# Differential attention: the output norm on other engines, its transposes later, the last head's products last

## The chip, the core and the metric

One kernel, one launch, on one core of a Trainium2 chip. TensorE (PE) multiplies and transposes into PSUM, which has eight banks of 128x512 float32 here; VectorE (DVE) and ScalarE (ACT) read PSUM and SBUF, GpSimd (POOL) only SBUF; SyncE (SP) issues every DMA of this kernel, in one queue. Each engine runs its instructions in the order in which they stand in the program. The metric is the device time of one execution in microseconds, the median of some runs.

## What is computed

One decoder layer: a normalised input is projected once, three branches (a convolution module, differential attention, cross-attention into memory tokens) are each gated and projected to the model width, summed under sigmoid gates, and projected once more. The change touches the differential attention and what follows it:

```python
def one_block(args):                       # 128 query rows, all 8 heads, two maps m of width 64
    ...
    p = jax.nn.softmax(s, axis=-1)
    a = (p[:, :, 0] - lam * p[:, :, 1]).astype(vt.dtype)
    return jnp.einsum("bhqk,bhkd->bhqd", a, vt)
...
o = rms_norm(o, subln_g) * (1.0 - lambda_init)       # per head, 128 wide
o = o.reshape(B, S, DIFF_WIDTH) * jax.nn.silu(gate)
return o @ w_proj
...
y = g[:, :, 0] * y_conv + g[:, :, 1] * y_diff + g[:, :, 2] * y_mem
x = x + y @ w_out[l]
```

SEQ and D_MODEL are 1024, there are 8 heads. All is float32; each large product is made of three passes on float32r halves (high x high, low x high, high x low), the helper `mm3` on lines 78 to 80.

## The kernel before

The instructions of PE stand in the order in which the Python code writes them; those of the other engines and of SP are ordered by a scheduler, by priority and by its own estimate of times. A tile pool with `bufs=n` gives n buffers to a name in turn, and an instruction that takes a buffer again waits for the last reader.

**Attention** (lines 974 to 1369). The work is cut into 32 groups: 8 heads, and in each head four blocks `g` of 256 query rows in the order 2, 3, 0, 1. A group has these steps on PE, each with its helpers on other engines:

- scores (L1045, L1047) into two `sc` banks; DVE adds the distance and takes the maximum (L1051), DVE and ACT do the softmax (L1062 to L1069). `rc` is one over the sum of each map, and POOL copies its first column to `r` (the tile `r0`, L1071);
- transposes of the weights (L1089) into one of three `tp` banks, copied out by ACT (L1091);
- products with the values (L1097) into the one `av` bank, copied to the tile `o` by ACT (L1102);
- the output norm (L1106 to L1116): ACT sums squares (L1111), then the helper `rstd_of` makes one over the root: POOL L173, ACT L174 and L175, POOL L176 to L179, then POOL L1114 multiplies by `r`, and DVE scales `o` (L1116);
- the turn (L1118 to L1135): PE transposes `o` into a `tp` bank (L1123), ACT copies it out with a scale (L1126), POOL multiplies it by the gate `gd` (L1127), which a DMA fetched. For heads 0 to 3 the result is split into a high and a low half for the products below, for heads 4 to 7 it goes to memory (L1129).

At the start of each head POOL also makes the low halves of keys and queries (L1012) for the next one, and it makes low halves of weights (L113).

A planner walks a model of the engines' times and writes PE's steps in that order; `CHAIN` is the time that it allows between the squares of the norm and the scaled `o`, in its own units. Where no step is ready it inserts fill: six matmuls at a time of independent projections into two `mm` banks, evicted by DVE (L1162, L1191). So the fill's amount is fixed, and only its place moves.

**The end** (lines 1371 to 1418). The rest of the fill comes first, while the outputs of heads 4 to 7 are read back (L1378, tile `gin`) and split (ACT L83, DVE L84 into `GH` and `GL`). Then the projection of these four heads: 16 banks (two column halves `ci`, two row halves, four blocks `db`), each of 12 matmuls, in four `mm` banks by turns. Each bank is evicted by DVE: times the gate `sg` (L1404), plus the other branches (L1405, these summed by POOL on L1403), then split into `YH` (ACT L83) and `YL` (DVE L84). Last comes the output projection with `w_out`: 16 banks of 24 matmuls; the first of them needs the first row half of all eight blocks of `Y` (banks 1 to 4 and 9 to 12) and all eight slices of `w_out`, whose high halves ACT makes (L112) and whose low halves POOL (L113).

## Time and profile before

| | |
|---|---|
| median of 3 runs | 1714.31 us (1709.65 to 1719.4) |
| the profiled execution | 1716.81 us, of it a span of 1715.0 us |
| attention | about 1168.8 to 1562 us of the span |
| projection of heads 4 to 7 | 1574.6 to 1619.7 us |
| output projection | 1619.7 to 1711.2 us |
| PE busy | 1645.4 us, 96% |
| DVE, ACT, POOL busy | 76%, 54%, 48% |
| granted PE clock, mean | 0.986 of full |

PE works nearly all the time, so time goes where PE waits, and where it works at the lower of its two clock levels. A table of waits gives, per line of PE, what ended its idle time. A timeline gives single instructions with the idle time ahead of them in brackets. The granted clock of a stretch is 1.00 at the full level (2.4 GHz) and 0.50 at the lower one (1.2 GHz).

### The profile page before, as it was taken

Reading aid. Unit: us, or ns where it says so; the run is one execution under the profiler, and the core shown is the slowest. Engines: PE = TensorE matmul, PEld = TensorE weight load, DVE = VectorE, ACT = ScalarE, POOL = GpSimd, SP = SyncE. Lnnn points to the kernel's source line nnn. Section 1 sums busy time; section 2 is a strip of 40 time slices with the busy share of each in tenths; the row PEclk is TensorE's granted clock in tenths of the full one; section 3 lists DMA queues with packets and bytes.
Section 4 is the critical chain, followed back from the end, with each engine's and each line's share of the span. In section 5 each row is a group of like instructions: output and inputs, shape, how many; then the busy total and the mean of one; then the engine's idle time right before and its main releaser. Section 6 shows DMA issues by size and latency. Waiting matters only on the chain. (4 is left out here: it accounts for less than half of the span.)

```text
span 1715.0 us, 24253 instructions
## 1 busy us (share of the span) xinstructions
PE 1645.4 (96%) x7882; PEld 1365.9 (80%) x7882; DVE 1296.4 (76%) x2232; ACT 919.0 (54%) x1948; POOL 814.8 (48%) x859
## 2 busy tenths in 40 slices
PE   6999999979999999999999999998997999999999
PEld 5788888858888788888888878877886878877787
DVE  7969998987999999967667997834666677675911
ACT  5614645334444455665566886844766776763200
POOL 3320111689677775434233344246456574457820
PEclk8999999989999999999999999999998999999999
DMA  7410222322342344654454233497377465466632
GB/s 273 151 35 24 77 65 78 99 88 78 124 134 74 111 148 144 216 192 135 158 167 148 92 99 105 139 323 219 119 251 249 136 182 158 142 217 220 191 121 89
DMA packets 201399, 247.51 MB, mean 144 GB/s; under 512 B 15377, under 2 KB 109590, under 8 KB 201272
## 3 DMA queue, kind: packets, MB, share of 16 engines
q1 hardware_dynamic: 201272, 245.96, 44.5%
q8 instruction: 62, 1.02, 0.2%
q14 instruction: 65, 0.53, 0.1%
HBM read 172.50 MB, written 73.40 MB: 143 GB/s over the span
## 5 line engine op out<-in xcount | busy, mean ns | idle before, releaser
L422 DVE SCALAR_TENSOR_TENSOR cv<-u,cw,cv 128x512 f32<-128x512 f32 x464 | 349.2, 753 | 11.1
L113 POOL TENSOR_TENSOR wL<-wraw,wH 128x512 fp32r<-128x512 f32 x104 | 143.2, 1392 | 254.1 <-ACT wH L112 159.3
L78 PE MATMUL mm<-hH,wH 128*128 128x512 f32 x512 | 207.1, 405 | 0.6 <-DVE sg L1191 0.6
L79 PE MATMUL mm<-hL,wH 128*128 128x512 f32 x512 | 202.2, 395 | 0.0
L80 PE MATMUL mm<-hH,wL 128*128 128x512 f32 x512 | 202.1, 395 | 0.0
L623 ACT CAST wH<-wraw 128x512 fp32r<-128x512 f32 x190 | 115.6, 618 | 114.4 <-PE tp L642 44.7
L621 POOL TENSOR_TENSOR ws<-wraw,wraw 128x512 f32<-128x512 f32 x38 | 60.2, 1584 | 182.9 <-DVE wL L624 134.2
L1051 DVE CUSTOM_DVE_ANT_0 p<-sc,dist 128x512 f32<-128x512 f32 (+3 forms) x192 | 100.4, 551 | 58.4 <-PE sc L1047 57.9
L624 DVE TENSOR_TENSOR wL<-wraw,wH 128x512 fp32r<-128x512 f32 x128 | 106.3, 837 | 26.4 <-ACT wH L623 26.2
L1065 ACT ACTIVATE p<-p,nm 128x768 f32<-128x768 f32 (+7 forms) x128 | 98.3, 770 | 47.1 <-DVE nm L1063 46.9
L642 PE MATMUL tp<-hH,wH 128*128 128x512 f32 x304 | 119.4, 393 | 3.4 <-ACT sx L647 3.4
L642 PE MATMUL tp<-hH,wL 128*128 128x512 f32 x304 | 119.3, 392 | 0.4 <-DVE wL L624 0.4
L642 PE MATMUL tp<-hL,wH 128*128 128x512 f32 x304 | 119.1, 392 | 0.0
L80 PEld LDWEIGHTS mm<-hH,wL 128*128 128x128 f32 x512 | 97.5, 191 | 21.4
L78 PEld LDWEIGHTS mm<-hH,wH 128*128 128x128 f32 x512 | 97.5, 190 | 18.4 <-DVE sg L1191 0.8
L79 PEld LDWEIGHTS mm<-hL,wH 128*128 128x128 f32 x512 | 97.7, 191 | 17.7
L112 ACT CAST wH<-wraw 128x512 fp32r<-128x512 f32 (+1 forms) x112 | 64.4, 589 | 62.4 <-PE mm L80 33.8
L647 ACT COPY sx<-tp 128x512 f32<-128x512 f32 x152 | 88.2, 580 | 6.0 <-PE tp L642 5.0
L624 POOL TENSOR_TENSOR wL<-wraw,wH 128x512 fp32r<-128x512 f32 x62 | 84.4, 1371 | 14.1 <-ACT wH L623 13.9
L623 ACT CAST wH<-ws 128x512 fp32r<-128x512 f32 x76 | 47.0, 619 | 74.1 <-PE tp L642 61.1
L621 POOL TENSOR_TENSOR wraw<-wraw,ws 128x512 f32<-128x512 f32 x38 | 59.6, 1568 | 52.2 <-DVE wL L624 50.5
L1045 PE MATMUL sc<-k,q 128*128 128x512 f32 (+2 forms) x192 | 69.7, 370 | 9.5 <-DVE mx L1051 9.4
(323 smaller groups left out, 4765.5 us busy)
## 6 DMA issues: line engine op xcount, KB each, us to landing
wraw<-in_w_in_dram SPq DMA_DIRECT2D x184, 256.0 KB, 3.2
sg<-sgT SPq DMA_DIRECT2D x65, 256.0 KB, 3.3
sgT<-sx SPq DMA_DIRECT2D x48, 256.0 KB, 3.3
qf<-qT SPq DMA_DIRECT2D x32, 256.0 KB, 4.3
kf<-kT SPq DMA_DIRECT2D x32, 256.0 KB, 4.2
yT<-sg SPq DMA_DIRECT2D x32, 256.0 KB, 4.0
w<-cvT SPq DMA_DIRECT2D x20, 256.0 KB, 3.4
mw<-in_w_mem_kv_dram SPq DMA_DIRECT2D x16, 256.0 KB, 6.6
```

The lines of the kernel that those rows point to most:

```text
L78: nc.tensor.matmul(ps, lhsT=lh, rhs=rh, start=start, stop=False)
L79: nc.tensor.matmul(ps, lhsT=lh, rhs=rl, start=False, stop=False)
L80: nc.tensor.matmul(ps, lhsT=ll, rhs=rh, start=False, stop=stop)
L113: self.low(kk).tensor_tensor(L[:, :w], raw[:, :w], r2f(H[:, :w]), op=ALU.subtract)
L422: nc.vector.scalar_tensor_tensor(ps if j < CONV_K - 1 else acc, u[:, at - j:at - j + 512], cw[:, c, 30 - j:31 - j], ps, op0=ALU.mult, op1= ...
L621: nc.gpsimd.tensor_tensor(o, x, y, op=op)
L623: nc.scalar.copy(H, a)
L624: (nc.gpsimd if n in on_pool else nc.vector).tensor_tensor(L, a, r2f(H), op=ALU.subtract)
L642: nc.tensor.matmul(R[bank], lhsT=l[:, ks], rhs=r, start=start and k == 0 and i == 0, stop=stop and k == 3 and i == 2, skip_group_check=True)
L647: last[0] = nc.scalar.copy(R[n], R[bank])
L1051: nc.vector.tensor_tensor_reduce(out=pm[m][:, k0:k0 + w], in0=sc[m][:, :w], in1=dist[:, d0:d0 + w], scale=1.0, scalar=-3.0e38, op0=ALU.add ...
L1065: nc.scalar.activation(pm[m][:, :n], pm[m][:, :n], AF.Exp, bias=nm[:, m:m + 1], scale=slope, accum_out=sm[:, m:m + 1])
```

## The change

Five edits, with all matmuls and their sizes as before:

1. `r0` is no longer a tile that POOL fills; it is a list of the columns of `rc`, which gets 12 buffers.
2. The norm keeps one POOL instruction, the first (now L1113). ACT squares the estimate (L1116), DVE does the rest in two instructions (L1117, L1118), and the scaling of `o` takes both factors (L1121).
3. In the turn DVE reads PSUM, scales and multiplies by the gate in one instruction (L1131), in place of ACT and POOL.
4. The planner's `CHAIN` goes from 8.0 to 11.0, except for the last two groups; its model of the turn's copy moves from ACT to DVE.
5. At the end eight `mm` banks are open in place of four. The eight banks of the first column half get the products of heads 4, 5 and 6 first, all eight of them, then each the products of head 7 and its eviction. The second column half is as before.

```diff
-                            A["r0"] = new(tiny, [P, 2], "r0", bufs=4)
+                            A["r0"] = []
...
-                        rc = new(tiny, [P, 2], "rc")
+                        rc = new(tiny, [P, 2], "rc", bufs=12)
...
-                        nc.gpsimd.tensor_copy(A["r0"][:, t:t + 1], rc[:, 0:1])
+                        A["r0"].append(rc[:, 0:1])
...
-            rstd_of(y, ss, [P, 2], 1.0 / P, 1e-6, eps6, pool=tiny, tags=("onv", "ont"))
-            nc.gpsimd.tensor_tensor(y, y, A["r0"], op=ALU.mult)
+            nc.gpsimd.tensor_scalar(v, ss, 1.0 / P, 1e-6, op0=ALU.mult, op1=ALU.add)
+            nc.scalar.activation(x, ss, AF.Ln, bias=eps6[:, 0:1], scale=1.0 / P)
+            nc.scalar.activation(y, x, AF.Exp, scale=-0.5)
+            nc.scalar.activation(x, y, AF.Square)
+            nc.vector.scalar_tensor_tensor(x, x, -0.5, v, op0=ALU.mult, op1=ALU.mult)
+            nc.vector.scalar_tensor_tensor(y, x, 1.5, y, op0=ALU.add, op1=ALU.mult)
             for t in range(2):
-                nc.vector.tensor_scalar_mul(o[:, t * P:(t + 1) * P], o[:, t * P:(t + 1) * P], y[:, t:t + 1])
+                sl = slice(t * P, t * P + P)
+                nc.vector.tensor_scalar(o[:, sl], o[:, sl], y[:, t:t + 1], A["r0"][t], op0=ALU.mult, op1=ALU.mult)
...
-            nc.scalar.activation(oF, tp[:, :256], AF.Copy, scale=sg8[:, 0:1])
-            nc.gpsimd.tensor_tensor(oF, oF, gd, op=ALU.mult)
+            nc.vector.scalar_tensor_tensor(oF, tp[:, :256], sg8[:, 0:1], gd, op0=ALU.mult, op1=ALU.mult)
...
-                    t_of["o", n] = run("DVE", run("ACT", t_of["av", n], 0.17, 0.17) + CHAIN, 0.17, 0.17)
+                    t_of["o", n] = run("DVE", run("ACT", t_of["av", n], 0.17, 0.17) + (CHAIN if n < 30 else 8.0), 0.17, 0.17)
...
-        open_banks(mm=4)
+        open_banks(mm=8)
...
+        def open_bank(ci, db, sl, heads_):
+
+            ps = on_bank.setdefault((ci, db, sl.start), None) or mm_bank()
+            on_bank[ci, db, sl.start] = ps
+            for h in heads_:
+                H, L = Ws[ci]()[h - HD]
+                c = slice(db * P, db * P + P)
+                mm3(ps, H[:, c], L[:, c], Gd[h][0][:, sl], Gd[h][1][:, sl], h == HD, h == DH - 1)
+
+
+        for half, sl in halves():
+            for db in range(4):
+                open_bank(0, db, sl, range(HD, DH - 1))
...
-                    weave(bank_T(Ws[ci], db * P, lambda kk: (Gd[kk][0][:, sl], Gd[kk][1][:, sl]), done))
+                    if ci:
+                        open_bank(ci, db, sl, range(HD, DH))
+                    else:
+                        open_bank(ci, db, sl, range(DH - 1, DH))
+                    done(on_bank.pop((ci, db, sl.start)))
```

How the instructions stand at three places. First POOL around the norm of the ninth group (the first of the third head). `onv`, `ont` and `osy` are the norm's small tiles, `r` the copied factor, `kL` and `q` the low halves for the next head, `wL` those of weights. Before:

```order
L1012 TENSOR_TENSOR kL<-kf,k 128x512 x2
L1012 TENSOR_TENSOR q<-qf,q 64x512 x2
L1127 TENSOR_TENSOR oT<-oT,gd 128x256
L113 TENSOR_TENSOR wL<-wraw,wH 128x512 x2
L176 TENSOR_TENSOR ont<-osy 128x2
L1071 COPY r_12287<-rc 128x1
L113 TENSOR_TENSOR wL<-wraw,wH 128x512 x2
L1133 TENSOR_TENSOR oT<-oT,gd 128x256
L1071 COPY r_12483<-rc 128x1 x2
L177 TENSOR_TENSOR ont<-ont,onv 128x2
```

The same place after:

```order
L1137 TENSOR_TENSOR oT<-oT,gd 128x256 x2
L1012 TENSOR_TENSOR kL<-kf,k 128x512 x2
L1113 TENSOR_SCALAR onv<-oss 128x2
L1012 TENSOR_TENSOR q<-qf,q 64x512 x2
L113 TENSOR_TENSOR wL<-wraw,wH 128x512 x4
L1137 TENSOR_TENSOR oT<-oT,gd 128x256
```

The norm's four steps on POOL that stood between and behind the splits of the next head and of weights are gone from this queue, with the copies of `r`; only the first step is left.

Second, DVE near the end of attention, with a norm, a turn and the scores of the last head. Before:

```order
L1116 TENSOR_SCALAR o<-o,osy 128x128 x2
L1191 TENSOR_TENSOR sg<-mm,sg 128x512
L1116 TENSOR_SCALAR o<-o,osy 128x128 x2
L1051 ISA p_15294,mx<-sc,dist 128x384
```

After:

```order
L1131 SCALAR_TENSOR_TENSOR oT<-tp,sg_256,gd 128x256
L1117 SCALAR_TENSOR_TENSOR ont<-ont,onv 128x2
L1051 ISA p_15143,mx<-sc,dist 128x384
L1051 ISA mx 128x1
L1051 ISA p,mx<-sc,dist 128x384
L1051 ISA mx 128x1
L1118 SCALAR_TENSOR_TENSOR osy<-ont,osy 128x2
L1195 TENSOR_TENSOR sg<-mm,sg 128x512
L1062 TENSOR_TENSOR mx<-mx 128x2
L1121 TENSOR_SCALAR o<-o,osy,rc 128x128 x2
```

DVE has three more instructions per group, and they stand between those that empty the score banks.

Third, DVE at the end, from the splits of the last outputs on (`y` is the sum of the other branches, `YH` and `YL` the halves of the result). Before:

```order
L84 TENSOR_TENSOR GL<-gin,GH 128x512 x3
L1191 TENSOR_TENSOR sg<-mm,sg 128x512
L1404 TENSOR_TENSOR sg<-mm,sg 128x512
L1405 TENSOR_TENSOR sg<-sg,y_16089 128x512
L84 TENSOR_TENSOR YL<-sg,YH 128x512
```

After:

```order
L84 TENSOR_TENSOR GL<-gin,GH 128x512 x6
L1423 TENSOR_TENSOR sg<-mm,sg 128x512 x2
L1424 TENSOR_TENSOR sg<-sg,y_15977 128x512
L1423 TENSOR_TENSOR sg<-mm,sg 128x512
L1424 TENSOR_TENSOR sg<-sg,y_15989 128x512
```

The evictions (now L1423, L1424) keep their place behind the splits, but on PE the first of them now comes behind the products of three heads in all eight banks and of the fourth in one, 75 matmuls, where it came behind 12. On PE 42 fill matmuls are left behind the last turn, where 60 were.

## Rows read from the trace of the kernel before

**Rows 1.** The page, part 1: busy time of PE, share, instructions.

```profile
PE 1645.4 (96%) x7882; PEld 1365.9 (80%) x7882; DVE 1296.4 (76%) x2232; ACT 919.0 (54%) x1948; POOL 814.8 (48%) x859
```

**Rows 2.** Waits of PE, 1165 to 1563 us: total us, times, longest.

```profile
PE sc L1045 <- DVE mx L1051: 9.4, 9, 1.9
PE tp L1123 <- DVE o L1116: 8.5, 3, 6.3
...
PE mm L78 <- DVE sg L1191: 0.6, 1, 0.6
```

**Rows 3.** Waits of PE, 1563 to 1715 us.

```profile
PE mm L78 <- ACT wH L112: 1.2, 1, 1.2
PE mm L79 <- DVE GL L84: 0.8, 1, 0.8
PE mm L79 <- POOL wL L113: 0.8, 1, 0.8
```

**Rows 4.** Stretches: length, busy PE, PEld, DVE, ACT, POOL (instructions), clock, DMA.

```profile
1303.80:1310.60 6.80, 4.45 (x15) 3.79 (x16) 1.17 (x3) 1.22 (x3) 3.19 (x10) 0.50 1.07 333
...
1574.60:1624.60 50.00, 49.01 (x214) 39.65 (x212) 47.29 (x48) 12.99 (x22) 42.22 (x26) 1.00 0.73 239
1628.10:1631.50 3.40, 3.40 (x10) 2.66 (x9) 2.92 (x3) 1.16 (x3) 3.40 (x3) 0.50 0.47 154
```

**Rows 5.** Timeline of PE around the longest wait: start, us, instruction [idle before].

```profile
1299.20 0.63 PE L80 MATMUL mm<-hH,wL 128*128 128x512 f32 x1
1306.15 0.66 PE L1123 MATMUL tp<-ident,o 128*128 128x128 f32 x2 [6.32 <-DVE o L1116]
```

**Rows 6.** Timeline of POOL ahead of that wait.

```profile
1290.11 0.19 POOL L173 TENSOR_SCALAR onv<-oss 128x2 f32<-128x2 f32 x1
...
1300.54 0.37 POOL L176 TENSOR_TENSOR ont<-osy 128x2 f32<-128x2 f32 x1
...
1305.49 0.19 POOL L1114 TENSOR_TENSOR osy<-osy,r 128x2 f32<-128x2 f32 x1
```

**Rows 7.** Groups of POOL, 1200 to 1540 us: busy, mean ns | idle before.

```profile
L1127 POOL TENSOR_TENSOR oT<-oT,gd 128x256 f32<-128x256 f32 x29 | 24.0, 826 | 29.5 <-ACT oT L1126 28.9 <-PE mm L80 0.3
L1071 POOL COPY r<-rc 128x1 f32<-128x1 f32 x60 | 19.3, 323 | 56.2 <-DVE rc L1067 52.2 <-DMA sg<-sgT 3.0 <-DVE mx L1062 0.4
```

**Rows 8.** Groups of DVE, 1200 to 1540 us.

```profile
L1051 DVE CUSTOM_DVE_ANT_0 p<-sc,dist 128x256 f32<-128x256 f32 x30 | 11.7, 414 | 0.3 <-PE sc L1047 0.3
...
L1062 DVE TENSOR_TENSOR mx<-mx 128x2 f32<-128x2 f32 x28 | 7.9, 284 | 0.7
```

**Rows 9.** Group of ACT, 1200 to 1540 us: the turn's copy.

```profile
L1126 ACT ACTIVATE oT<-tp,sg 128x256 f32<-128x256 f32 x29 | 13.6, 469 | 15.1 <-PE tp L1123 14.2 <-issue 0.7
```

**Rows 10.** One long stretch of attention, columns as in group 4.

```profile
1200.00:1540.00 340.00, 320.30 (x1910) 276.88 (x1909) 231.14 (x705) 233.11 (x625) 189.54 (x356) 0.98 0.59 184
```

**Rows 11.** Timeline of PE: the last turn, and the first product of heads 4 to 7.

```profile
1559.93 0.38 PE L1123 MATMUL tp<-ident,o 128*128 128x128 f32 x2
...
1574.61 0.39 PE L78 MATMUL mm<-GH,wH 128*128 128x512 f32 x1
```

**Rows 12.** Timeline of DVE: the fourth and fifth split, the first eviction.

```profile
1572.56 2.38 DVE L84 TENSOR_TENSOR GL<-gin,GH 128x512 fp32r<-128x512 f32 x2
...
1580.05 0.68 DVE L1404 TENSOR_TENSOR sg<-mm,sg 128x512 f32<-128x512 f32 x1
```

**Rows 13.** Groups of POOL from the first eviction to the twelfth, 1580 to 1618.6 us.

```profile
L113 POOL TENSOR_TENSOR wL<-wraw,wH 128x512 fp32r<-128x512 f32 x8 | 13.4, 1685 | 1.8 <-ACT wH L112 1.8
L1403 POOL TENSOR_TENSOR y<-y,yH 128x512 f32<-128x512 f32 x7 | 11.6, 1670 | 0.4 <-DMA y<-yT 0.3
L1403 POOL TENSOR_TENSOR y<-y,yL 128x512 f32<-128x512 f32 x6 | 9.9, 1663 | 0.5 <-DMA y<-yT 0.5
```

**Rows 14.** Timeline of DVE: the sums of the twelfth and thirteenth bank.

```profile
1617.87 0.68 DVE L1405 TENSOR_TENSOR sg<-sg,y 128x512 f32<-128x512 f32 x1
...
1619.85 1.78 DVE L1405 TENSOR_TENSOR sg<-sg,y 128x512 f32<-128x512 f32 x1
```

**Rows 15.** Timeline of PE: the output projection resumes with the last slice of its weights.

```profile
1627.23 0.50 PE L79 MATMUL mm<-wL,YH 128*128 128x512 f32 x1 [0.85 <-POOL wL L113]
```

More of the change, by code (lines that the diff above doesn't have):

```diff
@@ L1100, in prod @@
                 if jp == g:
-                    A["o"] = new(ap_, [P, 256], "o", bufs=4)
+                    A["o"] = new(ap_, [P, 256], "o", bufs=OB)
                     nc.scalar.copy(A["o"], A["av"][:, :256])
@@ L1108, in norm @@
             o, ss, y = A["o"], new(tiny, [P, 2], "oss"), new(tiny, [P, 2], "osy")
+            v, x = new(tiny, [P, 2], "onv"), new(tiny, [P, 2], "ont")
             junk = new(ap_, [P, P], "ojunk", bufs=1)
             for t in range(2):
-                nc.scalar.activation(junk, o[:, t * P:(t + 1) * P], AF.Square, scale=A["r0"][:, t:t + 1],
-                                     accum_out=ss[:, t:t + 1])
-            rstd_of(y, ss, [P, 2], 1.0 / P, 1e-6, eps6, pool=tiny, tags=("onv", "ont"))
-            nc.gpsimd.tensor_tensor(y, y, A["r0"], op=ALU.mult)
+                nc.scalar.activation(junk, o[:, t * P:(t + 1) * P], AF.Square, scale=A["r0"][t], accum_out=ss[:, t:t + 1])
+            nc.gpsimd.tensor_scalar(v, ss, 1.0 / P, 1e-6, op0=ALU.mult, op1=ALU.add)
[4 more added lines that the diff above has]
+            nc.vector.scalar_tensor_tensor(y, x, 1.5, y, op0=ALU.add, op1=ALU.mult)
             for t in range(2):
-                nc.vector.tensor_scalar_mul(o[:, t * P:(t + 1) * P], o[:, t * P:(t + 1) * P], y[:, t:t + 1])
+                sl = slice(t * P, t * P + P)
+                nc.vector.tensor_scalar(o[:, sl], o[:, sl], y[:, t:t + 1], A["r0"][t], op0=ALU.mult, op1=ALU.mult)
         def turned(h, g, A):
@@ L1137, in hybrid_layer @@
         ORDER, IDLE = (2, 3, 0, 1), 0.4
-        PARTS, SLACK, HOP, CHAIN, LOAD, AB, CHUNK, FIRST = 4, 1.25, 0.3, 8.0, 3.0, 3, 3.0, 11.0
+        PARTS, SLACK, HOP, CHAIN, LOAD, AB, OB, CHUNK, FIRST = 4, 1.25, 0.3, 11.0, 3.0, 3, 4, 3.0, 11.0
         def bank(W, b, r, c0, half, done, parts):
@@ L1286, in after @@
                     t_of["av", n] = run("ACT", at + HOP, 0.27)
-                    t_of["o", n] = run("DVE", run("ACT", t_of["av", n], 0.17, 0.17) + CHAIN, 0.17, 0.17)
+                    t_of["o", n] = run("DVE", run("ACT", t_of["av", n], 0.17, 0.17) + (CHAIN if n < 30 else 8.0), 0.17, 0.17)
                     t_of["done", h, g] = at
             needs = [("a", c), ("turn", h, jp // 2)] + ([("av", n - 1)] if n else []) + \
-                    ([("norm2", n - 4)] if jp == g and n > 3 else [])
+                    ([("norm2", n - OB)] if jp == g and n >= OB else [])
             return f, needs, lambda: 0.0, 4 * (384 if jp == g else 512) / 2400, after
@@ L1294, in after @@
             def after(at):
-                tps[0] = run("ACT", at + HOP, 0.36)
+                tps[0] = run("DVE", at + HOP, 0.36)
                 tps.append(tps.pop(0))
@@ L1390, in hybrid_layer @@
         Ws[0]()
+        on_bank = {}
+        def open_bank(ci, db, sl, heads_):
[8 more added lines that the diff above has]
+                open_bank(0, db, sl, range(HD, DH - 1))
         for ci in range(2):
```

## The prediction

> **What bounds the kernel now.** I read the page's busy times first: PE is busy 96% of the span [rows 1]. The change leaves every matmul as it is, so it can only move PE's idle time and the stretches at the lower clock. Then the waits of PE, for attention and for the end apart. In attention [rows 2] two lines matter: score matmuls that wait for DVE to empty a bank, 9.4 us in nine waits, and turns that wait for the scaled `o`, 8.5 us in three, one of them 6.3. At the end [rows 3] the waits are small: 0.8 us for a split of the last head's output, 2.0 us for the last slice of `w_out`. Then the granted clock by stretches [rows 4]: 0.50 behind the long wait of attention and again behind the wait at the end. Last the timelines of the longest wait: PE stands from 1299.8 to 1306.15 [rows 5], while POOL does the norm's first step at 1290.11, its second at 1300.54 and its last at 1305.49 [rows 6]. These are steps of about 0.2 us; the norm stood in POOL's queue behind splits for the next head and for weights.
>
> **Edits 1, 2 and 4, the norm and its room.** They take POOL's later steps out of that queue, and the turn stands about 3 us later in PE's order, with fill in the room. PE had fill to run in all three places, so I take the 8.5 us as gone [rows 2]. Behind the 6.3 us wait PE did 4.45 us of work at half clock [rows 4], which at full clock is half of that: 2.2 us gone too. What is late next there are the score banks, below. Both ends: nothing saved if the norm still comes late through its one POOL step or through DVE; 10.7 saved as taken. The list in place of `r0`, the 12 buffers of `rc` and the second factor of the scaling add no instruction: 64 copies leave POOL, and they cost nothing on PE before, since it never waits for them. ACT's new square is under the cover of its lost copies: it gives up 0.469 us per turn [rows 9]. Without that cover it would lengthen the norm by a few tenths, and the 3 us of room take that.
>
> **Edits 2 and 3 on DVE.** This is a price. DVE gets per group one read of 256 columns from PSUM, nearest row 0.414 us for the same size, and two tiny instructions with two inputs, nearest row 0.284 us [rows 8]. That is 0.98 us per group, 28 us for the 29 groups of the long stretch. POOL loses there 24.0 us of multiplying and 19.3 us of copies [rows 7], and the norm's steps, some 75 of its 190 us [rows 10]. Since DVE's instructions are lengthened where they meet POOL's (0.68 and 1.78 us for the same one [rows 14]), I give DVE 10 us back, an estimate: nine such meetings fewer. So DVE goes from 231 busy us of 340 [rows 10] to 249, its busy time from 2.1 times its idle time to 2.7. If the waits of the score matmuls grow like that ratio, 9.4 us become 12.2: 2.8 us lost. Ends: 4 gained, if less contention counts for more; 14.2 lost, if DVE takes over the waits that ACT had ahead of the turn's copy [rows 9], since everything behind L1131 in DVE's queue, score evictions above all, then waits for the turn and for the gate's DMA, and PE for them. I take 2.8, nearest to the row of the waits themselves.
>
> The Trainium skill (Advanced Engine Details and Errata, The Read-Write Bubble) says that ScalarE is closer to PSUM and VectorE to SBUF, which speaks against moving the turn's copy to DVE. The rows differ: 0.414 us on DVE beside 0.469 on ACT. By the page the new instruction would cost no less than ACT's, 1.8 us more DVE time over 32 groups, and the sum would grow by some 0.2 us.
>
> **Edit 5, the end.** Eight banks remove the 0.6 us wait of fill for a free bank [rows 2]. The last head's split costs 0.8 us before [rows 3], and that is all that putting its products last can win. What does it move? Call the end of the fill T, 1574.61 before [rows 11]. A matmul there takes 49.01 us / 214 = 0.229 us [rows 4]. Before, DVE's first eviction started at 1580.05 [rows 12], T + 5.4, and its twelfth sum ended at 1618.55 [rows 14], T + 43.9. From there a load, POOL's sixteenth sum and the last slice of `w_out` followed, and PE resumed at 1627.23 [rows 15], T + 52.6. This chain, and not PE, set the start of the output projection.
>
> After, the first eviction comes behind 75 matmuls, 17.2 us. Also, only 42 fill matmuls, 9.6 us, cover the reading back of heads 4 to 6, where 60 and a wait did before. The fifth split, head 6 in the first half, ended at 1574.94 [rows 12], 15.0 us after the last turn [rows 11]; the first bank now wants it 9.6 + 1.4 = 11.0 us after it. That is 4.0 us of waiting, so the first eviction starts at T + 21.2, 15.8 us later than before. Some of this comes back. Between the first and the twelfth eviction POOL ran 21 instructions with those of the evictions and weights [rows 13] and one of the fill; six or seven of them (two sums, a fill sum, three or four slices of weights) can now run ahead. A DVE sum took 1.78 us next to POOL and 0.68 alone [rows 14], 1.1 us for each meeting, so 6 x 1.1 = 6.6 us come back. The chain ends 9.2 us later against T, and PE, which has only 8 x 12 x 0.229 = 22 us of products behind the first column half, waits for it. Ends: 0, if evictions run at their bare rate; 15.8, if nothing comes back. I take 9.2; the rows of the same instructions give both parts of it. A wait of that length lowers the clock behind it: before, 3.40 us of work at half clock [rows 4], 1.7 us lost; after a longer wait, and with the one at the first bank, I take 1.0 us more, from 0 to 3.4.
>
> **The sum**, against the profiled execution of 1716.81 us: -8.5 - 2.2 + 2.8 - 0.6 + 9.2 + 1.0 = +1.7, so 1718.5. That execution stands 2.5 us over the median of the three runs, 1714.31, and the median is what I predict: 1716.0.
>
> **The rivals.** A, the end hides: DVE's evictions run bare, 12 banks x 3 x 0.68 = 24.5 us [rows 14], from T + 17.2 to T + 41.7, earlier than before, and PE never waits. Then 1716.0 - 9.2 - 1.0 = 1705.8. For it: POOL can work ahead. Against it: four buffers of `sg` and `y` let POOL run only four sums ahead, and it still has 14 or 15 instructions to run beside the twelve evictions.
>
> The Trainium skill (SBUF — State Buffer, SBUF: two separate sides) says that GpSimd and a VectorE instruction with two SBUF inputs share a port pair as an exclusive lock for a whole instruction. By that rule POOL's work there can be moved but not hidden, and A fails; the 1.78 beside 0.68 us agree.
>
> B, slower: DVE becomes the wait of attention. Place: L1131 ahead of the score evictions. Price: all 14.2 us of the turn's waits [rows 9] reach PE in place of 2.8, 1716.0 + 11.4 = 1727.4. It decides from about 10 us on. For it: the turn on PE is late in the order by design, and DVE then stands. Against it: the scheduler puts L1131 behind other work of DVE, and DVE is idle a quarter of the time.
>
> C, slower: nothing comes back at the end, 15.8 in place of 9.2: 1722.6. It decides if the reading back of heads 4 to 6 is later than before, because the last turn's gate is loaded late.
>
> D, the change does not do what it says: the norm is as late as before through its POOL step, now with DVE waiting for it, and 10.7 us stay: 1726.7. Against it: at the ninth group that step stands behind one pair of splits.
>
> **How the numbers follow.** Forecast 0.55, alone from 1709 to 1722; A 0.17, B 0.13, C 0.09, D 0.06. The predicted time is the forecast's, 1716. A measurement of this kernel tells about 0.5%, 8.6 us, from no change: below 1705.7 and above 1722.9. Half of A and a tail of the forecast lie below: 0.12. Most of B and D and half of C lie above: 0.17. The rest, 0.71, is within. For 8 in 10 the range reaches into A and to B: 1704 to 1727.
>
> **What would show it.** In the profile after: the turn's wait for `o` under 1 us in total and the clock at 1.00 around the third head (edits 1, 2, 4); score waits of 10 to 15 us (edit 3); 3 to 6 us of waits for `GL` in the first of the eight banks, the first L1423 some 21 us behind the last fill matmul, and 8 to 12 us of waits for `YL` or the last `wL` in the first bank of the output projection (edit 5). I am wrong if the output projection starts without such a wait (then A), if score waits pass 20 us (B), or if the turn still waits (D).

## The result and the profile after

The changed kernel took 1725.15 us, median of ten runs, beside 1714.14 us for the kernel before, also ten: a ratio of 1.0054, 95% interval 1.0040 to 1.0068. A second set, taken with the experiments, gave 1724.50 beside 1714.69: 1.0050 [1.0032, 1.0067]. So it is slower by half a percent, 10 to 11 us. The forecast was 1716.0, +1.7: the time lies in the range of 1704 to 1727, but above 1722, where the forecast by itself ended, and just over the line between "no change" and "slower".

The profiled execution took 1720.32 us, and its span is 1718.5, so this one is 4.8 us under the median of its kernel, where that of before is 2.7 over. Two spans are therefore a poor measure here (the last section shows why), and I compare stretches: from the first score matmul to the first product of the last four heads, and from there to the end. The first row of part 1 of the page after, against [rows 1]:

```profile
PE 1647.2 (96%) x7882; PEld 1371.0 (80%) x7882; DVE 1312.4 (76%) x2328; ACT 913.2 (53%) x1948; POOL 735.9 (43%) x603
```

PE's matmuls are the same 7882. The two stretches of after by windows, then its two stretches at half clock at the end (columns: window, length, busy time and instructions of PE, weight load, DVE, ACT, POOL, granted clock, DMA share, GB/s):

```profile
1169.80:1569.10 399.30, 377.95 (x2185) 327.05 (x2184) 295.16 (x876) 256.23 (x691) 165.57 (x156) 0.98 0.60 185
1569.10:1714.70 145.60, 136.90 (x577) 110.74 (x575) 65.10 (x71) 21.61 (x37) 51.15 (x34) 0.95 0.42 143
1573.10:1579.90 6.80, 5.15 (x12) 4.08 (x13) 6.65 (x4) 0.62 (x1) 6.80 (x5) 0.50 1.02 369
1627.70:1634.50 6.80, 3.96 (x9) 3.14 (x10) 6.80 (x6) 1.68 (x4) 6.80 (x5) 0.50 0.36 119
```

and the same two stretches of before:

```profile
1172.90:1574.60 401.70, 378.75 (x2185) 325.01 (x2184) 268.09 (x782) 264.77 (x692) 234.93 (x410) 0.98 0.58 183
1574.60:1711.20 136.60, 133.52 (x577) 108.87 (x575) 64.92 (x69) 20.04 (x34) 54.90 (x35) 0.99 0.46 153
```

Attention became 2.4 us shorter, the end 9.0 us longer: +6.6 together, and +8.6 in a second execution of the changed kernel (e0 below). What is left up to the 10 to 11 us of the medians, these traces don't place. The waits of PE in attention after (in total, times, longest):

```profile
PE sc L1045 <- DVE mx L1051: 8.6, 9, 2.1
PE av L1097 <- ACT a L1091: 5.9, 2, 4.7
PE av L1097 <- ACT o L1102: 2.8, 3, 1.3
PE mm L78 <- DVE sg L1195: 2.0, 1, 2.0
PE tp L1089 <- DVE p L1069: 1.9, 1, 1.9
```

The 8.5 us of turns waiting for `o` [rows 2] are gone altogether, yet the sum is 21.2 us. In before it was 22.5, with these rows beside those of [rows 2]:

```profile
PE av L1097 <- ACT a L1091: 1.6, 3, 0.8
PE av L1097 <- ACT o L1102: 1.0, 2, 0.8
PE tp L1089 <- DVE p L1069: 0.8, 1, 0.8
PE tp L1089 <- ACT oT L1126: 0.6, 1, 0.6
```

The waits of PE at the end, after, against [rows 3]:

```profile
PE mm L79 <- DVE GL L84: 3.3, 2, 2.4
PE mm L79 <- POOL wL L113: 2.8, 1, 2.8
PE mm L78 <- ACT wH L112: 1.3, 1, 1.3
PE mm L80 <- DVE YL L84: 1.0, 1, 1.0
PE mm L78 <- ACT YH L83: 0.2, 1, 0.2
```

They are 8.6 us, where before had 2.8 [rows 3]: 5.8 more. The two stretches at 0.50, each around one of the longer waits, hold 5.15 + 3.96 us of work, half of which is lost, 4.6 us; before it was 3.40 us of work, 1.7 lost [rows 4]: 2.9 more. Together these are 8.7 of the 9.0 us.

### The profile page after: what moved, and what is told of

Read it like the earlier page. It is cut to its first block, busy times and chain, and to the rows that moved or that the text cites. A ratio compares the mean times of both kernels' runs of the same rounds, so it can differ in the third digit from the quotient of the medians.

```text
span 1718.5 us, 24086 instructions
## 1 busy us (share of the span) xinstructions
PE 1647.2 (96%) x7882; PEld 1371.0 (80%) x7882; DVE 1312.4 (76%) x2328; ACT 913.2 (53%) x1948; POOL 735.9 (43%) x603
## 4 chain that ended last, share of the span: by engine, by line
PE 79%; DVE 8%; DMA 5%; issue 3%; ACT 2%; POOL 2%; SPq 0%; DVEq 0%; POOLq 0%; ACTq 0%
PE tp L642 23%; PE sc L642 11%; PE mm L78 9%; PE mm L79 9%; PE mm L80 9%; PE mm L642 6%; PE av L1097 3%; PE sc L1045 1%; PE sc L1047 1%; DVE cv L422 1%; PE tp L1089 1%; DMA sg<-sgT 1%; DMA wraw<-in_w_x_proj_dram 1%; DVE p L1051 1%; DVE p L1069 1%
## 5 line engine op out<-in xcount | busy, mean ns | idle before, releaser
L623 ACT CAST wH<-wraw 128x512 fp32r<-128x512 f32 x190 | 117.0, 621 | 169.5 <-PE tp L642 85.1
L624 DVE TENSOR_TENSOR wL<-wraw,wH 128x512 fp32r<-128x512 f32 x128 | 100.4, 790 | 28.0 <-ACT wH L623 27.9
L79 PEld LDWEIGHTS mm<-hL,wH 128*128 128x128 f32 x512 | 97.5, 190 | 17.3
L1097 PEld LDWEIGHTS av<-v,a 128*128 128x128 f32 x576 | 73.4, 197 | 13.9 <-ACT a L1091 6.8
L1097 PE MATMUL av<-v,a 128*128 128x128 f32 x576 | 75.2, 282 | 8.8 <-ACT a L1091 5.9
```

The source lines that it names most:

```text
L79: nc.tensor.matmul(ps, lhsT=lh, rhs=rl, start=False, stop=False)
L623: nc.scalar.copy(H, a)
L624: (nc.gpsimd if n in on_pool else nc.vector).tensor_tensor(L, a, r2f(H), op=ALU.subtract)
L1097: nc.tensor.matmul(A["av"][:, t * P:t * P + P], lhsT=A["a", jp][:, c * P:c * P + P], rhs=T["v", j // 4][:, j % 4, :], start=j == 0 and t = ...
```

## The experiments

All runs in one table: medians, each beside runs of the kernel before on the same chip, and from the trace of each run's profiled execution the two stretches and, at the end, the first eviction and the first of POOL's last four slices of `w_out`'s first column half (its end), both counted from the first product, and the sum of PE's waits there (added up from rounded rows).

| run | edits | median, before beside it | ratio [95%] | attention, us | end, us | first eviction | slice | waits at the end |
|---|---|---|---|---|---|---|---|---|
| before | none | | | 401.7 | 136.6 | 5.4 | 52.6 | 2.8 |
| after | 1 to 5 | 1725.15, 1714.14 | 1.0054 [1.0040, 1.0068] | 399.3 | 145.6 | 23.8 | 61.4 | 8.6 |
| e0 | 1 to 5 again | 1724.50, 1714.69 | 1.0050 [1.0032, 1.0067] | 399.5 | 147.4 | 23.9 | 62.3 | 9.4 |
| e11 | 1, 2 | 1712.11, 1714.83 | 0.9973 [0.9954, 0.9993] | 402.0 | 135.4 | 5.3 | 51.4 | 2.3 |
| e6 | 1, 2, 4 | 1711.29, 1714.69 | 0.9973 [0.9956, 0.9990] | 395.7 | 137.3 | 4.9 | 53.3 | 3.1 |
| e9 | 1, 2, 4, planner line of 3 | 1718.20, 1714.83 | 1.0017 [0.9993, 1.0041] | 399.1 | 141.7 | 12.8 | 57.9 | 7.0 |
| e1 | 1 to 4 | 1717.94, 1716.30 | 1.0009 [0.9991, 1.0027] | 398.7 | 140.3 | 10.7 | 57.9 | 5.5 |
| e2 | 5 | 1720.36, 1716.30 | 1.0026 [1.0010, 1.0041] | 404.9 | 139.7 | 17.3 | 55.3 | 6.2 |
| e12 | 1, 2, 4, 5 | 1715.36, 1714.83 | 0.9993 [0.9972, 1.0013] | 396.8 | 138.9 | 17.3 | 54.7 | 5.6 |
| e4 | 1 to 5, sums early on POOL | 1721.20, 1716.30 | 1.0030 [1.0014, 1.0045] | 398.8 | 144.6 | 24.1 | 59.6 | 7.0 |
| e7 | 1 to 5, sums early on DVE | 1715.99, 1714.69 | 1.0001 [0.9984, 1.0019] | 399.2 | 139.6 | 24.4 | 53.5 | 5.6 |
| e5 | 1 to 4, sums early on POOL | 1718.07, 1716.30 | 1.0017 [1.0000, 1.0034] | 399.8 | 140.7 | 11.4 | 56.5 | 4.8 |
| e8 | 1 to 4, second half first | 1715.55, 1714.69 | 1.0001 [0.9985, 1.0016] | 396.3 | 140.6 | 10.1 | 56.5 | 4.9 |
| e10 | 1, 2, 4, 5, sums early on DVE | 1705.37, 1714.83 | 0.9946 [0.9929, 0.9964] | 397.7 | 133.2 | 22.3 | 50.8 | 1.9 |

The planner's line on the turn's copy, which stands above under edit 4, goes with edit 3 here: "1, 2, 4" is without it. The order of PE's instructions up to the first product is the same in before, e2 and e11, the same in after, e0, e1, e4, e5, e7, e8 and e9, and the same in e6, e10 and e12. So the column of attention shows how far executions differ: e2, whose attention is that of before instruction by instruction, took 404.9 us, and the eight with the order of after took 396.3 to 399.8.

### The two parts apart: e1, e2, e0

e1 is the changed kernel with the end of before; e2 is the kernel before with the changed end, the same lines the other way round. e0 is the changed kernel once more. e1 against after:

```diff
-        open_banks(mm=8)
+        open_banks(mm=4)
...
-        for half, sl in halves():
-            for db in range(4):
-                open_bank(0, db, sl, range(HD, DH - 1))
...
+                    weave(bank_T(Ws[ci], db * P, lambda kk: (Gd[kk][0][:, sl], Gd[kk][1][:, sl]), done))
```

> Edits 1 to 4 alone: norm, r0, the turn's copy on DVE and the later turns as after; the end (four banks, bank by bank) as before. Theory 1 (attention gains, the end loses): no waits of turns for o, first matmul of the end some 5 us earlier than before, time 1704 to 1710 us beside 1714 for before. Rival 2 (DVE's new load in attention costs what the norm gives back, and the profile of after was a lucky one): 1712 to 1720 us. Rival 3 (more stretches at half clock in attention): first matmul of the end as early as in after, but more than 41 us at half clock ahead of it, time 1712 or more.

> Edit 5 alone: eight banks, the last head's products last; attention as before. Theory 1: the whole loss is here, 1723 to 1730 us; first eviction 21 to 24 us behind the first matmul of the end and the output projection about 9 us later against it than before; two stretches of 6.8 us at half clock behind it. Rival 2 (the loss is in attention): 1712 to 1718 us.

> The changed kernel once more, beside the runs of the parts. If the two parts only add (1.6 us for edits 1 to 4, 4.1 us for edit 5, by their medians against before), it is 5 to 7 us over before; if the later splits of edits 1 to 4 and the late first eviction of edit 5 meet at the first bank, 8 to 12 us over it.

Edits 1 to 4 gain nothing: +1.6 us by the medians, within what can be told, where I had expected a gain. The time fits rivals 2 and 3; the half clock ahead of the first product, 51.0 us, is over the 41 of rival 3, but it is 44.3 before and 54.5 after, so it decides nothing. By the trace edits 1 to 4 save 3.0 us up to the first product and lose 3.7 at the end. Edit 5 alone costs 4.1 us, between the two theories, and its first eviction comes at 17.3 us and not at 21 to 24. Together the parts cost 9.8 to 11.0 us, not 5.7. By the medians that excess, 4 to 5 us, is not clear of the noise; by the traces the end grows by 3.7 and 3.1 us in the parts and by 9.0 and 10.8 in the whole, which says, as far as one or two traces tell, that they meet there. The one row of waits at the end of e1 shows where edits 1 to 4 lose:

```profile
PE mm L79 <- DVE GL L84: 5.5, 3, 2.4
```

That is the wait for the splits of the last heads, 0.8 us in before [rows 3], and a stretch at 0.50 stands around it in e1 too.

### Edits 1 and 2 alone: where the wait of the turns went (e11)

e11 against e1:

```diff
-            nc.vector.scalar_tensor_tensor(oF, tp[:, :256], sg8[:, 0:1], gd, op0=ALU.mult, op1=ALU.mult)
+            nc.scalar.activation(oF, tp[:, :256], AF.Copy, scale=sg8[:, 0:1])
+            nc.gpsimd.tensor_tensor(oF, oF, gd, op=ALU.mult)
...
-        PARTS, SLACK, HOP, CHAIN, LOAD, AB, OB, CHUNK, FIRST = 4, 1.25, 0.3, 11.0, 3.0, 3, 4, 3.0, 11.0
+        PARTS, SLACK, HOP, CHAIN, LOAD, AB, OB, CHUNK, FIRST = 4, 1.25, 0.3, 8.0, 3.0, 3, 4, 3.0, 11.0
...
-                tps[0] = run("DVE", at + HOP, 0.36)
+                tps[0] = run("ACT", at + HOP, 0.36)
```

> Edits 1 and 2 alone, the norm off POOL, with turns, copy, planner and end as before: PE's order is that of before, row by row. Theory 7a (the turns waited because the norm stood in POOL's queue): the 8.5 us of waits for o are under 1.5 us without any move of the turns; 1706 to 1711 us, or 1711 to 1714 if other waits take their place as they did with edit 4. Theory 7b (the room of edit 4 was needed): 4 us or more of waits for o stay, 1711 to 1715.

PE's order is here row by row that of before, so its waits can be laid side by side. Attention of e11:

```profile
PE sc L1045 <- DVE mx L1051: 12.6, 8, 5.4
...
PE tp L1128 <- DVE o L1121: 2.6, 2, 1.7
```

The turns wait 2.6 us instead of 8.5, and the scores 12.6 instead of 9.4 [rows 2]; attention is 402.0 us long, as before (401.7, and 404.9 in e2). By the wait this lies between the theories. The longest score wait, 5.4 us, ends at 1304.39, eight PE instructions ahead of the turn for which PE had stood 6.3 us [rows 5]. DVE's timeline there:

```profile
1298.36 0.17 DVE L1067 RECIPROCAL rc<-sm 128x2 f32<-128x2 f32 x1 [2.18 <-ACT p L1065]
1298.52 0.98 DVE L1117 SCALAR_TENSOR_TENSOR ont<-ont,onv 128x2 f32<-128x2 f32 x1
...
1299.60 1.12 DVE L1118 SCALAR_TENSOR_TENSOR osy<-ont,osy 128x2 f32<-128x2 f32 x1
1300.64 1.27 DVE L1069 SCALAR_TENSOR_TENSOR p<-p,c,p 128x1024 f32<-128x1024 f32 x1
1301.84 1.96 DVE L1121 TENSOR_SCALAR o<-o,osy,rc 128x128 f32<-128x128 f32 x2
...
1303.80 0.53 DVE L1051 CUSTOM_DVE_ANT_0 p<-sc,dist 128x384 f32<-128x384 f32 x1
```

The norm's last steps stand in DVE's queue ahead of the eviction (1303.80) that frees the score bank, and its two tiny steps take 0.98 and 1.12 us there, beside POOL's splits of the next head. The norm is no longer late for the turn; it makes the evictions late. The ratio of 0.9973 says that a little is left of the gain (2.7 us), but this profiled execution shows none of it in attention. e6, which adds the room of edit 4, has the same ratio: by the medians the room gains nothing that can be told, though attention is 4 to 6 us shorter than in e11 in the traces with it (e6, e10, e12).

### Edit 3: the copy, or the planner's line on it (e6, e9)

e6 leaves edit 3 out: copy, gate product and planner line as before. e9 leaves out the copy alone and keeps the planner's line, and with it PE's order of e1, row by row. Against e1, the first hunk in both, the second in e6 alone:

```diff
-            nc.vector.scalar_tensor_tensor(oF, tp[:, :256], sg8[:, 0:1], gd, op0=ALU.mult, op1=ALU.mult)
+            nc.scalar.activation(oF, tp[:, :256], AF.Copy, scale=sg8[:, 0:1])
+            nc.gpsimd.tensor_tensor(oF, oF, gd, op=ALU.mult)
...
-                tps[0] = run("DVE", at + HOP, 0.36)
+                tps[0] = run("ACT", at + HOP, 0.36)
```

> Edits 1, 2 and 4 without edit 3: the turn's copy stays on ACT and the gate's product on POOL; the end as before. Theory 4a (the copy on DVE makes the reading back of heads 4 to 7 late): splits of the last heads end 19 to 20 us behind the last turn, as before, in place of 24, waits for GL under 2 us, time 1712 to 1716. Theory 4b (they are late because the last turn stands later against the fill, with 45 matmuls of fill behind it where there were 63): the same waits for GL of 5 us and the half clock behind them, 1716 to 1720.

> Edits 1 to 4 with PE's order exactly as in the run of edits 1 to 4, but the turn's copy on ACT and the gate's product on POOL as before; the end as before. Theory 8a (edit 3 costs by DVE's new instruction itself): 1710 to 1713 us, splits of the last heads early. Theory 8b (it costs by the order that its planner line gives PE: 45 matmuls of fill behind the last turn): waits for GL of about 5 us and 10 us at half clock as in the run of edits 1 to 4, 1715 to 1719.

e6 is 3.4 us under before, e9 3.4 us over it (its runs scatter more than the others', from 1706.8 to 1725.8), and their intervals don't touch; between them is one line of the planner. e1 and e9, which differ in the engine of the copy alone, can't be told apart (1.7 us between them, and some 5 either way are within the noise); the new instruction took 478 ns on DVE in after, the copy alone 469 on ACT in e9. So it was theory 8b: what edit 3 cost came mainly from the order, and no cost of DVE's new instruction shows. By the traces 3.4 us of it lie in attention and 4.4 at the end. The stretch from the last turn to the first product, e6:

```profile
1539.80:1561.70 21.90, 21.90 (x99) 18.15 (x98) 15.13 (x16) 8.12 (x15) 15.09 (x11) 1.00 0.88 300
```

and e9:

```profile
1550.80:1563.20 12.40, 10.15 (x45) 7.76 (x43) 1.40 (x3) 3.58 (x6) 10.11 (x11) 1.00 0.70 205
```

The stretch holds 99 PE instructions in e6, 63 in before and 45 in e9, e1 and after, all but three or four of them fill. The last split of the last head ends 20.6 us behind the start of the last turn in e6, 26.9 in e9; e6 has fill for 21.9 us of that and not one wait for a split. The first waits of the end of e9:

```profile
PE mm L79 <- DVE GL L84: 4.6, 4, 1.7
PE mm L78 <- ACT GH L83: 2.4, 2, 1.4
```

Why the line has this effect is argued from the code and not tried: the planner adds the copy to DVE's backlog, holds scores back by that backlog, and puts fill into the holes it sees, so that less is left for the end.

### The end: what the eight banks cost (e12, e4, e7, e10)

e12 is the end of after behind e6's attention. Against after:

```diff
-            nc.vector.scalar_tensor_tensor(oF, tp[:, :256], sg8[:, 0:1], gd, op0=ALU.mult, op1=ALU.mult)
+            nc.scalar.activation(oF, tp[:, :256], AF.Copy, scale=sg8[:, 0:1])
+            nc.gpsimd.tensor_tensor(oF, oF, gd, op=ALU.mult)
...
-                tps[0] = run("DVE", at + HOP, 0.36)
+                tps[0] = run("ACT", at + HOP, 0.36)
```

> The changed kernel without edit 3: copy and planner on ACT, the end as after. If edit 5 costs only its late evictions when the splits are there in time, 3 to 5 us over the run of edits 1, 2 and 4, 1714 to 1717 us, first eviction 17 us behind the first matmul of the end and no waits for GL. If it costs by itself what it cost in the changed kernel, 8 us: 1719 us or more.

It is 0.5 us over before and so 3.9 over e6, though the intervals of the two overlap, and its end is only 1.6 us longer: with the splits there in time, the order of edit 5 costs no more than about what it costs on before (4.1). With late splits it costs 8.2 to 9.4 (e0 and after, less e1).

The columns of the table show how. In nine of the ten runs whose projection waits for POOL's slice (before, after, e0, e2, e4, e6, e8, e11, e12) the end comes 84.0 to 85.1 us behind that slice: 136.6 - 52.6 = 84.0 before, 145.6 - 61.4 = 84.2 after. In the tenth, e10, it comes 82.4 us behind, with no half clock there. So where PE waits for the slice, what moves the slice moves the end. From e6 to e12 it moves by 1.4 us, from e12 to after by 6.7, and there the first eviction comes 6.5 us later, 23.8 in place of 17.3: with eight banks open nothing is full until each of the heads but the last has been in each of them, so the waits for splits push the first eviction back, and the whole chain behind it. With four banks the same late splits move the slice by 4.6 us (e6 to e1) and the end by 3.0; in e1 PE itself is so late that it doesn't wait for the slice.

The chain itself, DVE in after from the first eviction on:

```profile
1592.88 1.43 DVE L1423 TENSOR_TENSOR sg<-mm,sg 128x512 f32<-128x512 f32 x2 [13.12 <-PE mm L80]
...
1597.97 0.68 DVE L84 TENSOR_TENSOR YL<-sg,YH 128x512 fp32r<-128x512 f32 x1
1598.58 0.68 DVE L1424 TENSOR_TENSOR sg<-sg,y 128x512 f32<-128x512 f32 x1
1599.18 5.17 DVE L84 TENSOR_TENSOR YL<-sg,YH 128x512 fp32r<-128x512 f32 x3
1604.27 0.68 DVE L1423 TENSOR_TENSOR sg<-mm,sg 128x512 f32<-128x512 f32 x1
```

DVE stands 13.1 us while PE opens the banks; then the same split takes 0.68 us or 5.17 / 3 = 1.72. What ends PE's longest wait of the projection in after is POOL's slice of `w_out`, which stands behind its sixteen sums:

```profile
1627.55 1.26 POOL L1422 TENSOR_TENSOR y<-y,yL 128x512 f32<-128x512 f32 x1 [0.45 <-DMA y<-yT]
1628.77 6.79 POOL L113 TENSOR_TENSOR wL<-wraw,wH 128x512 fp32r<-128x512 f32 x4
```

So three runs take the sums out of there: e4 does them in place in the partial sums, still on POOL, eight beside the last fill and eight behind it; e7 does them on DVE, most of them ahead of the first eviction; e10 is e7 with e6's attention. e7 against after (e4 has `nc.gpsimd` in the fourth line):

```diff
+        def add_c(d, sl):
+            y0 = new(dp, [P, 512], "y0", bufs=8)
+            nc.sync.dma_start(y0, yT[1][d * P:d * P + P, sl])
+            nc.vector.tensor_tensor(partial(d, sl), partial(d, sl), y0, op=ALU.add)
...
-                        nc.gpsimd.tensor_tensor(y0, y0, partial(d, sl), op=ALU.add)
                         nc.vector.tensor_tensor(sg, ps, sg, op=ALU.mult)
-                        nc.vector.tensor_tensor(sg, sg, y0, op=ALU.add)
+                        nc.vector.tensor_tensor(sg, sg, partial(d, sl), op=ALU.add)
```

> The changed kernel with POOL's sixteen sums y0 + partial taken out of the evictions: done in place in the partial sums, eight beside the last fill and eight behind it, while PE opens the banks. Same result. Theory 1a (the end waits for the chain of evictions, which DVE and POOL share sum by sum): twelfth eviction 8 to 12 us earlier against the first matmul of the end, waits for YL and the last wL gone or under 1 us, time 1713 to 1718 us beside 1725. Rival 1b (the wait is for the late first eviction and the last head's splits alone): no more than 3 us gained, 1722 to 1726.

> The changed kernel with the sixteen sums y0 + partial on DVE in place of POOL, ahead of the first eviction, in the 13 us in which DVE stands while PE opens the banks. Theory 5a (the evictions are slow because POOL's sums stretch DVE's): twelfth split of Y 6 to 9 us earlier against the first matmul of the end than the 58.5 us of after, waits of the output projection under 2 us, time 4 to 8 us under after. Theory 5b (they are slow by POOL's slices of w_out and by the four buffers of sg): twelfth split at 55 to 58 us, within 3 us of after.

> Edits 1, 2 and 4 (copy and planner on ACT) with the changed end and its sixteen sums on DVE ahead of the first eviction. If the late first eviction is paid back by evictions free of POOL's sums, and the splits are there in time: no waits for GL, end 133 to 136 us behind its first matmul in place of 137.3, 1706 to 1711 us. If not: as the run of edits 1, 2 and 4 or up to 4 us over it, 1711 to 1715.

On POOL but earlier (e4), the end is 1.0 us shorter by the profile and the median stands 4.9 over before instead of 9.8: between the theories, and the intervals of e4 and e0 overlap. On DVE (e7) it is 6.0 us shorter, and the median 8.5 under that of e0: theory 5a by the time. But the twelfth split of Y, which 5a wanted at some 50 us, ends at 57.4, 1.1 earlier than in after; what moved is POOL's last four slices of `w_out`, whose first ends at 53.5 us in place of 61.4. In e7 this released it:

```profile
1623.63 0.62 ACT L83 CAST YH<-sg 128x512 fp32r<-128x512 f32 x1 [1.61 <-DVE sg L1430]
1624.15 0.62 ACT L112 CAST wH<-wraw 128x512 fp32r<-128x512 f32 x1
...
1624.90 6.38 POOL L113 TENSOR_TENSOR wL<-wraw,wH 128x512 fp32r<-128x512 f32 x4 [21.16 <-ACT wH L112]
```

POOL stands idle for 21.2 us ahead of the slice. What it waits for is the cast `wH` of the same slice, and that stands in ACT's queue behind the splits `YH`: behind the eleventh in e7, where it starts at 51.5 us, and behind the thirteenth in after (57.4) and in e4 (57.2); the thirteenth split itself starts at 55.8 in e7 and at 56.9 in after. So e4 shows what POOL's sums do to the slice by standing ahead of it, 1.8 us (61.4 to 59.6). The other 6.1 us of e7 came with the earlier place of the cast in ACT's queue, which the scheduler chose and which was not tried by itself. Before, the slice did not wait for a sum either:

```profile
1625.90 6.35 POOL L113 TENSOR_TENSOR wL<-wraw,wH 128x512 fp32r<-128x512 f32 x4 [2.41 <-ACT wH L112]
```

What the sums do to DVE's own instructions, e10 and e12 show. DVE's groups in the stretch of the evictions, e12 (1580.4 to 1616.0; busy, mean ns):

```profile
L84 DVE TENSOR_TENSOR YL<-sg,YH 128x512 fp32r<-128x512 f32 x13 | 16.2, 1261 | 0.0
L1425 DVE TENSOR_TENSOR sg<-sg,y 128x512 f32<-128x512 f32 x14 | 13.0, 936 | 0.2
```

and e10 (1586.9 to 1616.0):

```profile
L84 DVE TENSOR_TENSOR YL<-sg,YH 128x512 fp32r<-128x512 f32 x13 | 9.8, 766 | 0.0
...
L1431 DVE TENSOR_TENSOR sg<-sg,yH 128x512 f32<-128x512 f32 x8 | 6.5, 820 | 0.1
L1431 DVE TENSOR_TENSOR sg<-sg,yL 128x512 f32<-128x512 f32 x6 | 4.1, 684 | 0.0
```

The same instructions take 766 ns instead of 1261, and 684 to 820 instead of 936, with fewer POOL instructions beside them. The chain from the first eviction to the twelfth split takes 26.8 us in e10 and 34.1 in e12, so that e10 is done 2.3 us earlier, though it starts 5.0 later. Its waits at the end are 1.9 us and no stretch at half clock is left there: 133.2 us. e10 is 0.54% faster than before, the fastest of all: edits 1, 2, 4 and 5, and the sums on the engine that stands idle in any case. A run with the sums on DVE and four banks is missing, so it is not shown that edit 5 is needed for this gain.

The Trainium skill (SBUF — State Buffer, SBUF: two separate sides) says that GpSimd and a VectorE instruction with two SBUF inputs exclude each other for a whole instruction. e10 against e12 agrees: 1261 to 766 ns. e4 agrees too: POOL works off its sums and splits until 1605.3 us and then stands until 1625.0, and DVE's splits there are

```profile
1600.67 5.18 DVE L84 TENSOR_TENSOR YL<-sg,YH 128x512 fp32r<-128x512 f32 x3
...
1609.55 0.68 DVE L84 TENSOR_TENSOR YL<-sg,YH 128x512 fp32r<-128x512 f32 x1
```

### Two edits to e1's end (e5, e8)

e5 is e1 with the early sums of e4. e8 is e1 with the second half of the rows ahead of the first, because the very last turn belongs to the first half. e8 against e1:

```diff
-                    [lambda c=c, sl=sl: load(c, sl) for c in Gd for _, sl in halves()])
+                    [lambda c=c, sl=sl: load(c, sl) for _, sl in reversed(list(halves())) for c in Gd])
...
-            for half, sl in halves():
+            for half, sl in reversed(list(halves())):
...
-            for sb in range(NS):
+            for sb in (4, 5, 6, 7, 0, 1, 2, 3):
```

> Edits 1 to 4 with the end as before, but POOL's sixteen sums early as in the run of the same kind with eight banks. Theory 1a: the end's one wait (about 2 us for the last slice of w_out) goes too: 2 to 4 us under the run of edits 1 to 4 alone, 1701 to 1707 us. Rival 1b: same as edits 1 to 4 alone.

> Edits 1 to 4 with the end as before, bank by bank in four banks, but the second half of the rows first: its last turns are two groups earlier, the very last turn belongs to the first half. Theory 6a (what edits 1 to 4 lose at the end is the wait for the last head's splits and the half clock behind it): waits for GL under 1.5 us, no stretch at half clock behind the first matmul of the end, end 135 to 137 us behind it in place of 140.3, time 1711 to 1715. Theory 6b (it is the chain of evictions): 139 to 141 us, 1716 to 1719.

e5 gives nothing (end 140.7 beside 140.3): with four banks the sums are not what PE waits for, theory 1b. In e8 the waits for `GL` fall from 5.5 to 2.2 us and the half clock behind them goes, as 6a said, but the end is 140.6 us long, as 6b said: waits of 2.7 us for evictions and `w_out` came in their place, and the end lies 84.0 us behind POOL's slice. Its median is 0.9 us over before and can't be told from e1.

## Why the prediction was off by nine microseconds

That the time lies in the range is luck: the forecast by itself went up to 1722, and the range went on to 1727 for rivals whose mechanisms did not come. Against the sum of +1.7 the two stretches of after came to +6.6 and those of e0 to +8.6; the attention terms were off by some 6 us, the end by -1.2 and +0.6, and the rest lies between the traces and the medians.

**The turns' wait: gone, for a part of its price.** I wrote that PE had fill to run in all three places and that the 8.5 us were gone, and they are gone. The step that failed is "what is late next there are the score banks", with 2.8 us for it: the whole of attention came to -2.4 us (-2.2 in e0) where my terms for it add up to -8.5. In e11 what was late next was indeed the score bank, but eight instructions ahead of the old wait and by nearly the same time, 5.4 us, because the norm now stood on DVE. In after it was something I had not looked at: ACT. Its timeline at the longest wait of attention after, 1389.0 to 1393.66:

```profile
1389.03 0.28 ACT L1114 ACTIVATE ont<-oss,eps 128x2 f32<-128x2 f32 x1
1392.41 0.62 ACT L112 CAST wH<-wraw 128x512 fp32r<-128x512 f32 x1 [3.10 <-DMA wraw<-in_w_conv_proj_dram]
1392.94 0.20 ACT L1115 ACTIVATE osy<-ont 128x2 f32<-128x2 f32 x1
1393.04 0.56 ACT L1091 COPY a<-tp 128x512 f32<-128x512 f32 x1
```

A weight slice whose load has not landed stands at the head of ACT's queue, behind it the next step of the norm, and behind that the copy `a` for which PE waits. SyncE issued that load at 1386.05, so it was on its way for 6.3 us. In every run with the order of after the longest wait for `a` is 3.5 to 4.7 us (after, e0, e1, e4, e5, e7, e8, e9); in e6's order it is 1.8. That ties it to the order; an earlier load alone was not tried.

**The clock behind it: not given back.** I took 2.2 us for the stretch at half clock behind the 6.3 us wait. The clock at the third head is at its full level in after, as I said, but a stretch of 6.8 us at 0.50 came up at 1392.2, in the wait that began at 1389.0; in e1, e4 and e7, with the same order, 3.4 us at 0.50 stand at the third head too. Attention has 0.98 in both windows.

**Edit 3 on DVE: a price, but a larger one and for another reason.** I had 2.8 us of score waits, up to 14.2 by rival B. Score waits came to 8.6 us (9.4 in e0), no more than before and under the 10 to 15 that I had named, and between e9 and e1 the copy's engine makes no difference that can be told. The cost, 6.8 us between e6 and e9, sits in the planner's line: I read it as bookkeeping and asked only whether the turn was late, not how much fill it would leave behind the last turn. I had that number, 42 matmuls against 60, and charged it to edit 5 alone.

**Edit 5: the size as worked out, one link of the chain not.** The first eviction came 23.8 us behind the last fill (21.2 forecast), the waits for `GL` were 3.3 us (4.0), POOL's slice, with which PE resumed the projection, ended at 61.4 us (61.8), and the end grew by 9.0 us in one execution and 10.8 in the other (9.2 + 1.0). The waits of the projection were 5.3 us and not the 8 to 12 I named: PE comes later itself, slowed by the first bank and the half clock around its wait, so less of the delay is left to see there. The clock took 2.9 us more than before where I had 1.0. That POOL's sums make DVE's chain slow, e10 and e12 show (26.8 beside 34.1 us); e7, with four of the sixteen sums still inside the chain, is only 1.8 us faster than after (33.0). The link that I had wrong is the one from the chain to the slice: I put POOL's sixteenth sum ahead of it, but before it waited 2.4 us for ACT's cast `wH`, which stood behind a split `YH` in ACT's queue. In after the sixteenth sum did come last, 1.7 us behind the cast. What I had not seen is that the cost seems to come from two edits at once: without the order of edit 3 it is 3.9 us by the medians and 1.6 by the profiles, with it 8.2 and 5.3 or more.

**The rivals.** A (the end hides) did not happen. B named the median within 2.3 us, by a mechanism that is not there. C's sign came, a later reading back (the last split 22.7 us behind the last turn, before 19.6), but not its price: from the first eviction to the twelfth split it took 34.8 us, before 39.9, and POOL's slice ended 8.8 us later, not 15.8. D's idea, a norm that is late for someone else through DVE, is what e11 shows, on the score banks and not the turn.

**The method.** I moved the sum from one profiled execution to the median by the offset of the profile before, 2.5 us. The profile after stands 4.8 us on the other side, so two single spans would have shown +3.5 us for a change of 10 to 11.

## What to carry to other kernels

A wait that ends is worth its length only if the next instruction of every engine in front of that matmul is early too; before a wait is booked as gain, read the queues of all engines at that place for what comes second, here a weight slice on ACT and the norm's own steps on DVE. Where a planner spends filler work, count what it leaves for the one latency at the end that nothing else covers. And when many banks are opened before the first can be emptied, the evicting engine stands idle: that is the time in which to do its neighbour's work on it, and it was worth more (10 us between the medians of e12 and e10, 5.7 of them at the end by the profiles) than any of the five edits.

## What the hardware showed beside this

The instructions ahead of attention are the same in all these kernels, yet the first score matmul starts between 1164.1 us (e9) and 1173.9 (e0). Part of it lies in one stretch, 420 to 700 us; there e9, then e0 in the second fence:

```profile
420.00:700.00 280.00, 280.00 (x1237) 231.86 (x1236) 268.10 (x357) 143.47 (x255) 194.85 (x147) 1.00 0.41 129
```

```profile
420.00:700.00 280.00, 275.57 (x1212) 226.93 (x1211) 271.19 (x349) 134.70 (x242) 195.59 (x146) 1.00 0.39 124
```

At the same granted clock one execution runs 25 more matmuls in it. PE's waits there are none in e9 and in e0 this one row:

```profile
PE tp L642 <- ACT sx L647: 4.4, 3, 2.9
```

The same instructions fall into a wait or past it. A profile of a kernel of this length says what a stage costs, and several runs say what the kernel costs; one does not stand for the other. And the granted clock fell to 0.50 around waits as short as 2.4 us (1572.34 to 1574.75 in after, with one of 0.9 us ahead of it): at the end of this kernel 8.6 us of waits took 4.6 us of clock with them, and before the change 2.8 us of waits took 1.7 [rows 3, 4].
